# A hybrid decoder layer: four places of TensorE's planned order are made due three microseconds later

## The chip, the core and the metric

The kernel runs on one core of a Trainium2 chip. The metric is the time of one execution in microseconds of the device; lower is better. TensorE (PE in the rows) multiplies matrices, VectorE (DVE), ScalarE (ACT) and GpSimd (POOL) do the elementwise work, SyncE (SP) issues most DMAs. Weights are loaded into TensorE by a second queue, PEld.

## What is computed

One layer over 16 meta tokens and 512 tokens of 1024 channels: an RMSNorm, one projection into 11 blocks of columns, two mixers side by side, an output projection, another RMSNorm, and a mixture of 32 SwiGLU experts of which every token takes two. The first mixer is RWKV-7, a recurrence over tokens, which the kernel computes in chunks of 64 tokens:

```python
def step(S, inp):
    r_t, d_t, k_t, v_t, a_t, b_t = inp
    Sa = jnp.einsum('bhvk,bhk->bhv', S, a_t)
    S = S * d_t[:, :, None, :] + Sa[..., None] * b_t[:, :, None, :] + v_t[..., None] * k_t[:, :, None, :]
    return S, jnp.einsum('bhvk,bhk->bhv', S, r_t)
...
h = h + jnp.concatenate([y_a, y_b], axis=-1) @ w_out[l]
xn = _rmsnorm(h, norm_ffn_w[l])
h = h + _hmoe(xn, ...)     # top-1 of 4 groups, then top-2 of 8 experts, SwiGLU
```

The second mixer is an mLSTM, also in chunks. The weights of all 32 experts are read, as 16 pairs of experts with 12 tiles of 1 MB each (8 named `wgu`, 4 named `wdn`).

## The kernel before

**Stages.** (1) Projections: blocks of 128 columns, each 48 matmuls of 264 columns (three products of high and low parts, `proj_k`), in the order of `PLAN`: K, R and V blocks of the RWKV mixer (four each, numbered j = 0 to 3), then v, q, gate and o blocks of the others. (2) Between them the RWKV mixer for each j: `decays` (two groups of 6 matmuls), `norms`, `heads` (VectorE, ScalarE and GpSimd build the operands `Bbd`, `Kbd`, `MV`, one buffer of each for all four j), `products(j)` (two halves g = 0, 1 of 16 matmuls of 64x192, then two of 128x80), and `valued(j)`, which turns the values (4 matmuls of 128x128 and one of 16x128). (3) `inverse`: when the products of j = 3 are made (mark `P3`), VectorE inverts the chunks' triangles in a long row of dependent steps (`interleaved`); then TensorE does four times 32 matmuls of 32x32, two times after `need(Y2)`, two times after the copies `Zs`. (4) `chain`: nine steps over the chunks (`removals`, `solved`, `next_state`, `outputs`), with projections and the mLSTM in between. (5) The variances, the gate, the last projections (o), the output projection `w_out` (needs the token rows `x`, loaded by `residuals`), the router and the gather. (6) The experts, from L2072 on: each pair multiplies its 12 tiles as they land.

**Order.** Stages 1 to 5 are written by a planner that runs while the program is built. Each piece of work is a generator (a stream) with a rank, and `Weave.run` always resumes the stream of the lowest rank that isn't waiting. `Clock` estimates when each tensor is written; `need(...)` holds a stream back until the estimate of its operands, plus `LAG` and (for ranks above 0) `SLACK`, is reached; `bank(...)` does the same for a PSUM bank. While one stream is held back, others place their matmuls. The estimate decides only the order: on the chip each instruction waits by semaphores for what it really needs. The order of TensorE and SyncE is that in which the streams issue; the instructions of VectorE, ScalarE and GpSimd are ordered by the framework's scheduler, which sees the order of the other two. All these instructions bear line 308, that of the recording helper, so in the rows they are told apart by shape: 128x264 on arS with arR or arQ is a projection, 64x192 the products, 128x80 their last two, 128x264 on arR alone the decays, 128x128 on arF `valued` or another transposition, 32x32 the inverse.

**What hangs on the order.** The low part of each block of weights is made by VectorE until `P3` is marked and by GpSimd afterwards (`lo_by` in `prepare`). Tiles are given addresses in the arenas by the planner's clock too, and so the tiles of expert weights: `prefetch` fetches them as room appears (from the mark `var` on), `residuals` takes room for `x`, and in the experts' loop `fetch` puts each further tile into the room that has been free longest, so the tiles go round in a ring.

## Time and profile before

| | |
|---|---|
| median of 3 runs | 904.93 us (900.92 to 907.99) |
| the profiled execution | 904.07 us |
| its span, first to last instruction | 902.3 us |
| TensorE busy | 826.9 us (92%) |
| VectorE / ScalarE / GpSimd busy | 434.1 / 264.3 / 203.1 us |
| TensorE's granted clock over the span | 0.958 |
| read from HBM | 234.38 MB |

The profiled execution takes 1.8 us more than its span. A busy TensorE is one that has a matmul under way, which is not the same as one at its peak. The granted clock is a share of 2.4 GHz; the two levels are 1.0 and 0.5.

### The profile page before, as it was taken

How to read it: one execution, taken by the hardware profiler on the slowest of the kernel's cores; microseconds unless marked ns; L12 is line 12 of the kernel's file. 1: busy time of each engine (PE TensorE's matmuls, PEld its weight loads, DVE VectorE, ACT ScalarE, POOL GpSimd, SP SyncE). 2: the span in 40 equal slices, each digit the busy share in tenths (PEclk: the TensorE clock that was granted, in tenths of full speed). 3: DMA queues.
4: the chain of work that ended last, by engine and by line, in shares of the span. 5: the costliest groups of instructions: out<-in, count | busy, mean ns of one | idle time of the engine just before them, and what ended most of it. 6: DMA issues, size and time to landing. Idle time of an engine off the chain costs nothing. (4 is left out here: it accounts for less than half of the span.)

```text
span 902.3 us, 13658 instructions
## 1 busy us (share of the span) xinstructions
PE 826.9 (92%) x5487; PEld 499.0 (55%) x5488; DVE 434.1 (48%) x819; ACT 264.3 (29%) x505; POOL 203.1 (23%) x278
## 2 busy tenths in 40 slices
PE   7989697878899889999999999999999999999994
PEld 5878596777887767888343444433444423332331
DVE  7677757598746639437132333423333323331324
ACT  5755555634345584312110111001110101001102
POOL 5164625365543328220100000000000000000002
PEclk8988889988998899999999999999999999999998
DMA  6210111311300222989999999999999999999982
GB/s 238 71 42 7 47 63 55 83 34 38 102 25 2 74 84 72 386 329 348 376 406 393 419 420 420 420 420 420 420 420 420 420 421 420 420 419 422 421 349 97
DMA packets 45142, 235.60 MB, mean 261 GB/s; under 512 B 9906, under 2 KB 10290, under 8 KB 21008
## 3 DMA queue, kind: packets, MB, share of 16 engines
q1 hardware_dynamic: 42192, 228.58, 63.6%
q0 software_dynamic: 2160, 3.93, 1.1%
q10 hardware_dynamic: 720, 2.15, 0.6%
q8 instruction: 45, 0.74, 0.3%
q14 instruction: 25, 0.20, 0.1%
HBM read 234.38 MB, written 4.19 MB: 264 GB/s over the span
## 5 line engine op out<-in xcount | busy, mean ns | idle before, releaser
L308 PE MATMUL accs<-arS,arR 128*128 128x264 f32 (+2 forms) x1136 | 180.8, 311 | 8.3 <-DVE arS L308 3.5
L308 PEld LDWEIGHTS accs<-arS,arR 128*128 128x128 f32 (+1 forms) x1136 | 160.6, 199 | 22.4 <-issue 5.5
L308 PE MATMUL accs<-arF 64*64 64x192 f32 (+17 forms) x1361 | 112.6, 289 | 29.8 <-DVE arF L308 20.0
L2072 PE MATMUL accs<-arF 128*64 128x512 f32 x568 | 133.2, 599 | 6.2 <-DMA arF<-wgu 6.1
L2000 DVE TENSOR_TENSOR arF<-arF,accs 128x512 f32<-128x512 f32 x124 | 80.8, 683 | 100.4 <-PE accs L1998 98.9
L308 PEld LDWEIGHTS accs<-arF 64*64 64x64 f32 (+6 forms) x1346 | 83.1, 157 | 46.3 <-DVE arF L308 15.9
L308 POOL TENSOR_TENSOR arF<-arF 128x528 f32<-128x528 f32 (+13 forms) x97 | 89.9, 929 | 83.1 <-DVE arF L308 56.6
L1809 POOL DMA_INDIRECT arM<-hd,arF x15 | 15.1, 1008 | 372.8 <-DVE arF L1799 356.1
L308 DVE TENSOR_TENSOR arF<-arF 64x16 f32<-64x16 f32 (+31 forms) x170 | 90.2, 578 | 7.4 <-POOL arF L308 4.7
L2072 PEld LDWEIGHTS accs<-arF 128*64 128x64 f32 x568 | 37.5, 137 | 87.1 <-issue 65.3
L308 ACT ACTIVATE arF<-arF 128x528 f32<-128x528 f32 (+7 forms) x113 | 59.8, 550 | 74.7 <-DVE arF L308 51.5
L2107 ACT ACTIVATE arF<-accs,arF 128x512 f32<-128x512 f32 x16 | 11.0, 687 | 240.1 <-PE accs L2072 240.1
L308 POOL TENSOR_SCALAR arF<-arF 64x256 f32<-64x256 f32 (+9 forms) x101 | 56.9, 565 | 95.3 <-ACT arF L308 43.2
L2140 DVE SCALAR_TENSOR_TENSOR arO<-accs,arF,arO 128x1024 fp32r<-128x1024 f32 x15 | 19.3, 1284 | 103.2 <-ACT arO L2139 103.2
L2130 PE MATMUL accs<-arF 128*64 128x512 f32 x280 | 63.8, 597 | 0.2 <-DMA arF<-wdn 0.2
L1997 PE MATMUL accs<-arO,OHT 128*128 128x512 f32 x124 | 57.5, 464 | 0.0
L308 ACT COPY arF<-accs 64x256 f32<-64x256 f32 (+7 forms) x111 | 39.8, 370 | 53.8 <-PE accs L308 28.2
L308 DVE TENSOR_TENSOR arF<-accs,arF 128x128 f32<-128x128 f32 (+7 forms) x81 | 35.6, 460 | 29.0 <-PE accs L308 21.1
L1998 PE MATMUL accs<-arO,OHT 128*128 128x512 f32 x124 | 49.0, 395 | 0.0
L308 PE MATMUL accs<-arW,arS 128*128 128x512 f32 x192 | 46.7, 398 | 0.0
L1997 PEld LDWEIGHTS accs<-arO,OHT 128*128 128x128 f32 x124 | 23.3, 188 | 40.4 <-issue 38.1
L2139 ACT ACTIVATE arO<-accs,arF 128x1024 fp32r<-128x1024 f32 x15 | 16.7, 1113 | 98.7 <-PE accs L2130 98.7
(142 smaller groups left out, 930.3 us busy)
## 6 DMA issues: line engine op xcount, KB each, us to landing
arF<-wgu SPq DMA_DIRECT2D x71, 1024.0 KB, 19.8
arF<-wdn SPq DMA_DIRECT2D x35, 1024.0 KB, 19.8
arM<-wgu SPq DMA_DIRECT2D x23, 1024.0 KB, 20.0
arH<-wgu SPq DMA_DIRECT2D x17, 1024.0 KB, 19.8
arN<-wgu SPq DMA_DIRECT2D x16, 1024.0 KB, 18.6
arF<-wb SPq DMA_DIRECT2D x23, 512.0 KB, 3.6
arM<-wdn SPq DMA_DIRECT2D x10, 1024.0 KB, 20.5
arN<-wdn SPq DMA_DIRECT2D x8, 1024.0 KB, 20.4
```

The costliest lines, as they stand in the source:

```text
L308: r = f(*args, **kw)
L1809: nc.gpsimd.indirect_dma_start(out=xt[p % 2], out_offset=None, in_=hd, in_offset=bass.IndirectOffsetOnAxis(ap=idx[:, p % 2:p % 2 + 1], axi ...
L1997: P.matmul(pq, lhs, oh[:, hs], start=True, stop=False)
L1998: P.matmul(pq, lhs, ol[:, hs], start=False, stop=True)
L2000: V.tensor_tensor(hv, hv, pq, op=OP.add)
L2072: P.matmul(pgu[64 * e:64 * e + 64, h], x[:, k, 64 * e:64 * e + 64], w[:, D * e + 512 * h:D * e + 512 * h + 512], start=(k == 0), stop=(k = ...
L2107: S.activation(av, pgu[:, 0], AF.Silu, scale=r1_)
L2130: P.matmul(pdn[64 * e:64 * e + 64, h], aT[:, k, 64 * e:64 * e + 64], w[:, D * h + 512 * e:D * h + 512 * e + 512], start=(k == 0), stop=(k ...
L2139: S.activation(oh, pdf, AF.Copy, scale=g1_)
L2140: V.scalar_tensor_tensor(ol, pdf, g1_, oh.bitcast(F32), op0=OP.mult, op1=OP.subtract)
```

## The change

`need` takes an additional time, `late`, that is added to the estimate, and three callers give it `LATE = 3.0`: the values' turn in `valued`, both halves of `products`, and the first two blocks of matmuls in `inverse`. In the diff they stand in this order. `Clock` itself is not changed, so what comes behind is estimated from the later places.

```diff
+LATE = 3.0
...
-    def need(self, *aps):
+    def need(self, *aps, late=0.0):
         while True:
-            t = self.clock.wrote(*aps) + self.clock.LAG + self.slack()
+            t = self.clock.wrote(*aps) + self.clock.LAG + self.slack() + late
             if t <= self.clock.t + 0.05:
                 return
             yield t
...
-        yield from need(v)
+        yield from need(v, late=LATE)
...
-            yield from need(Bbd, Kbd, MV)
+            yield from need(Bbd, Kbd, MV, late=LATE)
...
-            yield from need(Y2)
+            yield from need(Y2, late=LATE)
```

The diff adds one line near the top, so line 308 is 309 in the changed kernel. What it does to the engines' orders is seen best at four places.

**TensorE, behind the products of j = 1.** 128x80 and 128x512 end the products and the head of j = 1; the two rows of 128x264 on arR are the decays of j = 3, 128x264 on arF is `norms`, 128x128 `valued` of j = 0, and arS with arR or arQ are projections. Before:

```order
L308 MATMUL accs<-arF 128x80 x2
L308 MATMUL accs<-arF 128x512
L308 MATMUL accs<-arR 128x264 x6
L308 MATMUL accs<-arS_68,arR 128x264 x2
L308 MATMUL accs<-arS_70,arR 128x264 x2
L308 MATMUL accs<-arS_68,arQ 128x264 x2
L308 MATMUL accs<-arR 128x264 x6
```

The changed kernel:

```order
L309 MATMUL accs<-arF 128x80 x2
L309 MATMUL accs<-arF 128x512
L309 MATMUL accs<-arR 128x264 x6
L309 MATMUL accs<-arF 128x128 x4
L309 MATMUL accs<-arF 16x128
L309 MATMUL accs<-arR 128x264 x6
```

The values' turn of j = 0 now stands between the two groups of decays; the norms of j = 3 have gone ahead of the products of j = 1.

**VectorE, at the same place.** 128x16 from accs is the last read of the bank of the 128x80 products; the 64x512 and 64x16 rows build the operands of j = 2. Before:

```order
L308 TENSOR_TENSOR arF<-accs,arF 64x16
L308 TENSOR_TENSOR arF<-arF 64x512
L308 TENSOR_TENSOR arF<-arF 64x16
L308 TENSOR_TENSOR arF<-arF 64x512
L308 TENSOR_TENSOR arF<-arF 64x16
L308 TENSOR_TENSOR arF<-accs,arF 128x16
```

The changed kernel:

```order
L309 TENSOR_TENSOR arF<-accs,arF 64x16
L309 TENSOR_TENSOR arF<-accs,arF 128x16
L309 TENSOR_TENSOR arF<-arF 64x512
L309 TENSOR_TENSOR arF<-arF 64x16
L309 TENSOR_TENSOR arF<-arF 64x512
L309 TENSOR_TENSOR arF<-arF 64x16
```

The read that frees the bank comes ahead of the four operations that build operands, no longer behind them.

**TensorE, at the inverse.** Before, 24 projections stand between its two halves:

```order
L308 MATMUL accs<-arF 32x32 x64
L308 MATMUL accs<-arS_68,arR 128x264 x2
...
L308 MATMUL accs<-arS_69,arR 128x264 x2
L308 MATMUL accs<-arF 32x32 x64
```

The changed kernel:

```order
L309 MATMUL accs<-arS_69,arR 128x264 x2
L309 MATMUL accs<-arF 32x32 x128
L309 MATMUL accs<-arS_69,arR 128x264 x2
L309 MATMUL accs<-arS_71,arR 128x264 x2
L309 MATMUL accs<-arS_69,arR 128x264 x2
L309 MATMUL accs<-arF 16x64 x8
```

The 24 projections have gone ahead of the inverse, and 6 of the 12 that stood ahead of the chain's first step (16x64) have gone behind it.

**SyncE, around the token rows.** `wgu` and `wdn` are expert weights, `wo` the output projection's, `glb` the gate's, `x` the token rows. Before:

```order
L308 DMA arF<-glb 128x512
L308 DMA arF<-glb 32x512
L308 DMA arF<-wgu 128x2048
L308 DMA arF<-wo 128x512 x10
L308 DMA arF<-x 128x1024 x4
L308 DMA arF<-wgu 128x2048 x2
```

The changed kernel:

```order
L309 DMA arF<-wgu 128x2048
L309 DMA arF<-glb 128x512
L309 DMA arF<-glb 32x512
L309 DMA arF<-wo 128x512 x10
L309 DMA arF<-wgu 128x2048 x4
L309 DMA arF<-x 128x1024 x4
```

Four tiles of expert weights go ahead of the token rows, and the first one ahead of the gate's weights. Farther down in the same queue, from the second pair of experts on, a tile's address comes back after 15 tiles in the changed kernel and after 16 before; the final norm's weights (`nlw`) and one half tile of the last pair's `wdn`, which stood at the end of the queue, stand ahead of the first pair.

Counted along TensorE's rows, from the K block of j = 2 on (behind the decays of j = 1), this many projection matmuls stand ahead of each place:

| ahead of | before | changed |
|---|---|---|
| products j = 0, first half | 48 | 54 |
| products j = 1, first half | 144 | 210 |
| products j = 2, first half | 318 | 300 |
| products j = 3, first half | 432 | 402 |
| products j = 3, last two (mark `P3`) | 474 | 432 |
| values' turn j = 3 | 564 | 576 |
| inverse, first half | 690 | 714 |
| inverse, second half | 714 | 714 |
| chain, first `removals` / first `solved` | 726 / 738 | 720 / 726 |

From the chain's second `solved` on the counts agree, and 144 projections are left when the chain is done in both.

## Rows read from the trace of the kernel before

**Rows 1.** The page's second part: TensorE's clock, the DMA engines' busy share in tenths, and what they moved, in 40 equal slices of the span (22.6 us each).

```profile
PEclk8988889988998899999999999999999999999998
DMA  6210111311300222989999999999999999999982
GB/s 238 71 42 7 47 63 55 83 34 38 102 25 2 74 84 72 386 329 348 376 406 393 419 420 420 420 420 420 420 420 420 420 421 420 420 419 422 421 349 97
```

**Rows 2.** Busy time of each engine in four stretches of the span. Columns: the stretch and its length in us; busy us (and instructions) of PE, PEld, DVE, ACT and POOL; granted clock, the DMA engines' share, GB/s.

```profile
62.00:173.00 111.00, 92.93 (x770) 80.21 (x768) 74.72 (x110) 57.81 (x114) 50.90 (x75) 0.89 0.16 54
173.00:219.00 46.00, 34.82 (x258) 32.61 (x259) 44.53 (x120) 17.93 (x45) 25.07 (x45) 0.93 0.19 51
427.00:714.00 287.00, 286.33 (x1484) 112.18 (x1482) 91.90 (x180) 31.00 (x41) 11.58 (x12) 1.00 1.01 413
714.00:870.00 156.00, 146.58 (x690) 53.34 (x688) 46.57 (x79) 14.86 (x20) 3.54 (x4) 1.00 1.01 420
```

**Rows 3.** TensorE's instructions in order of time, those that it stood idle for (and, without a wait, the norms of j = 3 at 116.46): start, duration, count, and in brackets the idle time before and the engine that ended it.

```profile
64.33 0.54 PE L308 MATMUL accs<-arF 64*64 64x192 f32 x2 [1.69 <-DVE arF L308]
66.29 3.51 PE L308 MATMUL accs<-arF 64*64 64x192 f32 x28 [1.43 <-DVE arF L308]
...
93.62 2.84 PE L308 MATMUL accs<-arF 64*64 64x192 f32 x32 [4.18 <-DVE arF L308]
108.22 0.99 PE L308 MATMUL accs<-arR 64*128 64x264 f32 x6 [1.83 <-ACT arF L308]
113.36 1.69 PE L308 MATMUL accs<-arR 64*128 64x264 f32 x6 [3.21 <-DVE arF L308]
116.46 4.05 PE L308 MATMUL accs<-arF 128*128 128x264 f32 x14
139.53 1.52 PE L308 MATMUL accs<-arF 64*64 64x192 f32 x28 [0.57 <-ACT arF L308]
144.23 1.54 PE L308 MATMUL accs<-arF 128*128 128x80 f32 x6 [1.53 <-ACT arF L308]
148.29 1.16 PE L308 MATMUL accs<-arF 128*128 128x128 f32 x8 [1.04 <-ACT arF L308]
150.87 0.57 PE L308 MATMUL accs<-arF 128*16 128x128 f32 x2 [1.42 <-DVE arF L308]
168.86 1.52 PE L308 MATMUL accs<-arF 64*64 64x192 f32 x28 [0.96 <-ACT arF L308]
175.75 1.48 PE L308 MATMUL accs<-arF 128*128 128x128 f32 x10 [2.40 <-ACT arF L308]
193.19 2.62 PE L308 MATMUL accs<-arF 128*128 128x128 f32 x10 [4.21 <-DVE arF L308]
...
218.87 3.80 PE L308 MATMUL accs<-arF 32*32 32x32 f32 x128 [3.41 <-DVE arF L308]
237.03 0.62 PE L308 MATMUL accs<-arF 64*16 64x64 f32 x16 [2.11 <-ACT arF L308]
```

**Rows 4.** The projections between 62 and 240 us, grouped: count, busy time, mean duration in ns, idle time ahead of them.

```profile
L308 PE MATMUL accs<-arS,arR 128*128 128x264 f32 x645 | 95.3, 301 | 0.7 <-POOL arR L308 0.7
L308 PE MATMUL accs<-arS,arQ 128*128 128x264 f32 x66 | 14.1, 297 | 0.0
```

**Rows 5.** VectorE in order of time behind the products of j = 1: the four 64x512 and 64x16 operations, then the read that frees the bank.

```profile
108.88 4.22 DVE L308 TENSOR_TENSOR arF<-arF 64x512 f32<-64x512 f32 x4
113.13 0.17 DVE L308 TENSOR_TENSOR arF<-accs,arF 128x16 f32<-128x16 f32 x1
```

**Rows 6.** VectorE in order of time from the end of the R block of j = 3 (its first row reads that block's sums) to the last operand of the products of j = 3.

```profile
155.19 0.71 DVE L308 TENSOR_TENSOR arF<-accs,arF 128x528 f32<-128x528 f32 x1 [1.82 <-PE accs L308]
...
157.97 0.69 DVE L308 TENSOR_TENSOR arF<-arF 128x512 f32<-128x512 f32 x1
```

**Rows 7.** ScalarE's copies `Zs` and TensorE's work between the halves of the inverse, in order of time.

```profile
224.63 1.06 ACT L308 COPY arF<-accs 32x512 f32<-32x512 f32 x2
...
222.61 4.71 PE L308 MATMUL accs<-arS,arR 128*128 128x264 f32 x24
227.25 3.80 PE L308 MATMUL accs<-arF 32*32 32x32 f32 x128
230.98 1.72 PE L308 MATMUL accs<-arS,arR 128*128 128x264 f32 x12
```

**Rows 8.** The same operation of VectorE twice, alone and beside GpSimd's copies, and one low part of a block of weights made by GpSimd within the inverse's stretch.

```profile
59.86 0.68 DVE L308 TENSOR_TENSOR arF<-arF 64x512 f32<-64x512 f32 x1 [2.84 <-POOL arF L308]
61.14 3.14 DVE L308 TENSOR_TENSOR arF<-arF 64x512 f32<-64x512 f32 x1
186.18 2.52 POOL L308 TENSOR_TENSOR arR<-arF,arR 128x1024 fp32r<-128x1024 f32 x1
```

**Rows 9.** SyncE's issues in order of time around the token rows and at the experts' start, the landing time of the token rows, and VectorE's first read of them.

```profile
359.31 1.75 SPq L308 DMA_DIRECT2D arF<-x  x4
...
469.18 0.33 SPq L1740 DMA_DIRECT2D arF<-wdn  x1
475.11 3.76 SPq L1740 DMA_DIRECT2D arF<-wgu  x3
...
DMA to landing us min/median/max: 3.5/5.5/7.4
...
379.93 0.69 DVE L308 TENSOR_TENSOR arF<-arF,accs 128x512 f32<-128x512 f32 x1 [4.95 <-PE accs L308]
```

## The prediction, made before the changed kernel ran

> **What bounds the kernel now.** I read the page's slices first [rows 1]: for the first sixteen the DMA engines are mostly idle, then they stand at 420 GB/s to the end. So the span has two parts, a front (stages 1 to 5) bound by something on the chip and the experts. The stretches tell more [rows 2]: from 427 to 714 us TensorE is busy 286.33 of 287 us, from 714 to 870 us 146.58 of 156 us with the DMA engines full. The experts are thus bound first by TensorE and later by the stream of weights. After their start each further tile is asked for when room comes free, as at 469.18 and 475.11 us [rows 9], and room comes free as pairs are multiplied; so the stream too hangs on the time at which the experts begin. I take it that a shift of the front's end passes to the end of the kernel one to one.
>
> In the front the bound is TensorE's order. From 62 to 173 us, the RWKV mixer's operands and products, TensorE is busy 92.93 of 111 us, VectorE 74.72, ScalarE 57.81 [rows 2]: no engine is full, and TensorE loses 18.1 us at waits. The order of time names them [rows 3]: products of j = 0 1.69 and 1.43, of j = 1 4.18, decays of j = 3 1.83 and 3.21, products of j = 2 0.57 and 1.53, values' turn of j = 1 1.04 and 1.42, products of j = 3 0.96, and 0.2 of small ones. From 173 us (`P3`) to the inverse at 218.87 us it is otherwise: VectorE is busy 44.53 of 46 us and TensorE 34.82 [rows 2]; the values' turns of j = 2 and 3 wait 2.40 and 4.21 us, and the inverse itself 3.41 us for VectorE [rows 3]. Behind it, `solved` waits 2.11 us at 237.03 [rows 3].
>
> **The change part by part.** No instruction is added: the same matmuls stand in another order. A projection costs (95.3 + 14.1) / (645 + 66) = 0.154 us [rows 4].
>
> *Before `P3`.* By the table of counts 432 projections stand ahead of it, 474 before: 42 fewer, -6.5 us. They go into the stretch that VectorE bounds, priced below.
>
> The waits before `P3`, one by one. Products of j = 0 have 6 more projections ahead (0.9 us): 3.1 becomes 2.1. Products of j = 1 have 66 more ahead, 10.2 us against a wait of 4.18: that wait goes. Decays of j = 3: at 113.36 us TensorE waits for the bank that VectorE reads at 113.13, behind 4.22 us of other operations [rows 5]; in the changed order that read stands ahead of the four, and the values' turn of j = 0 stands between the decays' two groups. 5.0 becomes about 1.5, the first wait, for ScalarE, less a little. Products of j = 2 and the values' turn of j = 1 get three us of the estimate more: 2.1 becomes 1.2 and 2.5 becomes 1.5, half kept, since ScalarE's and VectorE's queues aren't shorter. Products of j = 3 grow: their R block now ends only 18 projections (2.8 us) ahead of them, while its sums are read at 155.19 and the last operand is ready at 157.97 + 0.69 = 158.66 [rows 6], 3.5 us, and up to 5 us with the norms; I take 0.96 becomes 3.0. A half us for a bank and the small 0.2 stay. Together 18.1 becomes 10.0: -8.1 us. At best the waits fall to 4 (-14); at worst they all come back elsewhere (0), the first rival.
>
> *From `P3` to the inverse.* 66 projections more, 282 against 216, fill what TensorE idles there: 34.82 + 66 x 0.154 = 45.0 us of the 46 that VectorE needs. So the cover is nearly used up: whatever waits are left in the stretch beyond 1.0 us lengthen it. Of the 2.40 and 4.21 us at the values' turns I let 2 us stay, 1.0 of which shows: +1.0 us, bounds 0 and +4 (half of all waits).
>
> A price that weighs against the change: one low part of a block of weights is now made by GpSimd, for `P3` is marked earlier in the planner's order. Such a part takes 2.52 us at 186.18 us, and one operation of VectorE took 0.68 us alone and 3.14 beside GpSimd's work [rows 8]. If that befalls the inverse's steps, the stretch grows by at most 3.14 - 0.68 = 2.5 us; but GpSimd is already busy 25.07 of the 46 us there [rows 2] with VectorE's steps as long as they are, so I take 0 and keep 2.5 for the range.
>
> The Trainium skill, page *GPSIMD Engine Reference*, section "1. Specifications", says that GpSimd shares its SBUF interfaces with VectorE and that instructions of VectorE with two SBUF inputs contend with it. By it the move would cost VectorE time just where VectorE is the bound, and the sum below would end near 894 us. The two durations of rows 8 agree with the rule; that its price is paid within the inverse no row shows.
>
> *The inverse.* The 24 projections between its halves go ahead of it. That doesn't give 4.71 us [rows 7]: the second half needs ScalarE's copies, over at 224.63 + 1.06 = 225.69, and it began at 227.25. It can begin 1.6 us earlier, or 2.0 with the step of 0.4 by which the copies follow a TensorE that works on nothing else: -2.0 us, bounds 0 and -4.7.
>
> *The chain's first step.* 6 fewer projections ahead of `removals` (-0.9) and, of the 12 that stood between it and `solved`, 6 are left (12 to 6 by the table, covering a wait that is 2.11 now [rows 3]), while the 6 are done later anyway: I take +0.9 for the longer wait plus 0.8 for the rest, +1.7. Net +0.8 us. From the second `solved` on the counts agree, and so I change nothing there.
>
> *The token rows.* They are issued behind four more tiles. At 359.31 us they were issued [rows 9] and landed by 368 us, 1.75 + 7.4 later at most. Four tiles of 128 x 2048 floats (1.05 MB) take 2.5 us each at 420 GB/s [rows 1]: they land by 378 us, and VectorE first reads them at 379.93 [rows 9]. Hidden, with a margin of 2 us; without it, what is over goes to the end one to one.
>
> *The ring.* A tile's address comes back after 15 tiles, not 16, so one tile less is ahead when the experts start, and the stream is asked at 475.11 us where it was asked at 469.18 [rows 9]. The loss shows after 714 us, where the stream is the bound: one tile, +2.5 us, bounds 0 and +5.9 (the difference of the two issues).
>
> *The sum.* -6.5 - 8.1 + 1.0 - 2.0 + 0.8 + 2.5 = -12.3 us. The profiled execution took 904.07 us, 1.8 more than its span and 0.9 less than the median: 904.07 - 12.3 = 891.8, so 892 us. Bounds with the terms at their ends: 880 to 903.
>
> One gain is not in the sum. Over 62 to 173 us the granted clock is 0.89 and over 173 to 219 us 0.93 of full speed, over the experts 1.00 [rows 2]; the products before and after their waits run at such lower clock. A front with fewer gaps could get some of this back: 0.11 x 92.93 + 0.07 x 34.82 = 12.7 us is the whole of it.
>
> **The rivals.**
>
> *The waits come back.* TensorE's waits are for a chain through VectorE and ScalarE (operands of j, banks, operands of j + 1, one buffer for all four j). If this chain is what sets the time of `P3`, then taking 42 projections out just makes room for longer waits. For it: every wait in rows 3 ends on VectorE or ScalarE, and VectorE's operations stretch when GpSimd works [rows 8]. Against it: both are idle a third or half of the stretch [rows 2], and the wait at 113.36 comes from an order, not from a load [rows 5]. Then only the inverse's -2.0 and +0.8 and the ring's +2.5 are left: 904.07 + 1.3 = about 905 us.
>
> *Slower: products of j = 1 become late for all behind them.* The 66 projections more ahead of them take 10.2 us, and the norms of j = 3, also ahead now, 4.05 us at 116.46 or half of it at full clock, 2.0; against that stand 4.18 us of wait and the 1.0 saved at the products of j = 0: products of j = 1 come 7.0 us later. The operands' buffers are single, so the operands of j = 2 can be built only then; before, the products of j = 1 began at 93.62 and those of j = 2 resumed at 139.53 [rows 3], 46 us. The point from which it decides is whether this distance shrinks by those 7 us. By counts 18 projections fewer than before lie ahead of products of j = 2, so TensorE's own part of it falls by 84 x 0.154 = 12.9 us; if VectorE and ScalarE need all of the 46 us, it does not shrink, the same holds behind it, and `P3` comes 7.0 us later: 904.07 + 7.0 - 2.0 + 0.8 + 2.5 = about 912 us. Against it stands the idle third of VectorE.
>
> *More than forecast.* The sum's waits at their best (-14 for -8.1) and half of the clock's 12.7 us: 892 - 5.9 - 6.3 = about 880 us.
>
> That the change doesn't do what it says is out: the orders shown above have moved.
>
> **How the numbers follow.** Forecast near 892 us 0.50, waits back (905) 0.25, late products (912) 0.15, more gain (880) 0.10. One per cent, 9 us, is about what a measurement of this kernel can tell from no change; its bounds are 896 and 914. Faster by over 1%: four fifths of the forecast's chance and the fourth case, 0.40 + 0.10 = 0.50. Slower by over 1%: the third case where its bounds reach beyond 914 us, half of it, 0.07. The rest, 0.43, is within 1%. The range, 882 to 907 us, leaves out the third case but for its lower third (0.10), and most of the fourth (0.08): 0.18.
>
> **What would show it.** In the changed trace: products of j = 1 start with no wait; the second group of decays of j = 3 waits less than 1 us; `P3` falls near 159 us (173 less 14.6) and the inverse's first half near 205 (218.87 less 14.6, and 1.0 more); a VectorE busy nearly all of the time between; TensorE idle there under 3 us; the second half of the inverse 2 us nearer to the first; VectorE's first read of the token rows waiting for TensorE, not a DMA; the experts' start 15 us earlier, and the last pairs waiting for tiles a little more. The prediction is wrong if the distance from products of j = 1 to those of j = 2 stays 46 us, if the values' turns of j = 2 and 3 still wait for ScalarE and VectorE in a stretch that TensorE fills, or if the token rows land after 380 us less what the front gained: with the front 15 us earlier they are issued earlier too, but the four tiles ahead of them wait for room that the same front frees.

## The result, and the profile of the changed kernel

The changed kernel takes 913.58 us (median of 9 runs, 909.15 to 916.09) where the kernel before, beside it, takes 904.14: ratio 1.0112, 95% interval 1.0093 to 1.0131. It is slower by 9.4 us; faster by 12 was forecast. The profiled execution took 910.71 us, 2.9 less than the median; its span is 909.0, and so the table below accounts for 6.6 of the 9.4 us.

Where the time went is seen only when both spans are cut at the same places of the program. Each place below is the start of TensorE's first matmul there; `P3` is the end of the last products, "chain's end" that of its last matmul.

| stretch | before | changed | change | forecast |
|---|---|---|---|---|
| start to products of j = 0 | 62.10 | 60.68 | -1.4 | 0 |
| products of j = 0 to `P3` | 110.35 | 102.73 | -7.6 | -14.6 |
| `P3` to the inverse | 46.42 | 51.93 | +5.5 | +1.0 |
| first half of the inverse to the second | 8.38 | 6.33 | -2.0 | -2.0 |
| second half to the chain's first `solved` | 9.78 | 11.24 | +1.5 | +0.8 |
| chain | 72.28 | 76.48 | +4.2 | 0 |
| chain's end to the gate | 24.69 | 27.28 | +2.6 | 0 |
| gate to the output projection | 25.47 | 25.15 | -0.3 | 0 |
| output projection to the experts | 67.05 | 69.99 | +2.9 | 0 |
| experts | 475.78 | 477.19 | +1.4 | +2.5 |
| span | 902.3 | 909.0 | +6.6 | -12.3 |

At `P3` the changed kernel is 9.0 us ahead, at the chain's first step 4.1, at the chain's end level, and at the experts 5.3 behind. The stretches of the kernel before and then of the changed one (columns as in rows 2):

```profile
62.10:172.45 110.35, 92.28 (x768) 80.14 (x768) 74.44 (x109) 57.19 (x112) 50.80 (x75) 0.89 0.16 53
172.45:218.87 46.42, 35.25 (x254) 32.55 (x252) 44.58 (x121) 18.46 (x47) 25.07 (x45) 0.93 0.20 53
237.03:309.31 72.28, 66.99 (x975) 58.60 (x975) 46.99 (x94) 35.26 (x89) 30.40 (x52) 0.94 0.14 43
```

```profile
60.68:163.41 102.73, 87.59 (x720) 74.89 (x720) 73.76 (x107) 55.83 (x112) 50.75 (x75) 0.90 0.14 47
163.41:215.34 51.93, 43.12 (x321) 40.73 (x319) 46.71 (x122) 19.87 (x47) 30.23 (x47) 0.93 0.25 67
232.91:309.39 76.48, 72.25 (x1002) 63.76 (x1002) 45.88 (x96) 34.31 (x90) 29.46 (x50) 0.91 0.05 17
```

TensorE of the changed kernel in order of time, the rows that answer to [rows 3]:

```profile
101.50 1.53 PE L309 MATMUL accs<-arF 64*64 64x192 f32 x32
115.99 1.00 PE L309 MATMUL accs<-arR 64*128 64x264 f32 x6 [1.94 <-ACT arF L309]
117.31 2.61 PE L309 MATMUL accs<-arF 128*128 128x128 f32 x10 [0.32 <-DVE arF L309]
133.37 1.52 PE L309 MATMUL accs<-arF 64*64 64x192 f32 x28 [0.38 <-ACT arF L309]
151.62 2.84 PE L309 MATMUL accs<-arF 64*64 64x192 f32 x32 [3.07 <-DVE arF L309]
159.25 1.52 PE L309 MATMUL accs<-arF 64*64 64x192 f32 x28 [1.11 <-ACT arF L309]
189.85 3.87 PE L309 MATMUL accs<-arF 128*128 128x128 f32 x15 [5.20 <-DVE arF L309]
210.10 4.90 PE L309 MATMUL accs<-arS,arR 128*128 128x264 f32 x38 [2.71 <-POOL arR L309]
215.34 3.80 PE L309 MATMUL accs<-arF 32*32 32x32 f32 x128 [0.34 <-DVE arF L309]
221.67 3.83 PE L309 MATMUL accs<-arF 32*32 32x32 f32 x128 [2.53 <-ACT arF L309]
232.91 0.87 PE L309 MATMUL accs<-arF 64*16 64x64 f32 x16 [3.20 <-ACT arF L309]
336.67 0.79 PE L309 MATMUL accs<-arW 128*128 128x512 f32 x1 [6.73 <-ACT arW L309]
389.64 3.77 PE L309 MATMUL accs<-arF 128*128 128x40 f32 x32 [1.11 <-DVE arF L309]
393.23 8.08 PE L309 MATMUL accs<-arW,arS 128*128 128x512 f32 x27
```

The last three stand at the gate, at a half of the router, and at the output projection's matmuls behind it. The other engines and queues of the changed kernel at the places where it lost time:

```profile
164.85 2.39 POOL L309 TENSOR_TENSOR arR<-arF,arR 128x1024 fp32r<-128x1024 f32 x1 [9.09 <-ACT arR L309]
165.96 1.85 DVE L309 SCALAR_TENSOR_TENSOR arF<-arF 128x527 f32<-128x527 f32 x1
167.88 0.81 SPq L309 DMA_DIRECT2D arF<-eye  x2
172.69 3.68 DVE L309 TENSOR_TENSOR arF<-arF 128x31 f32<-128x31 f32 x11 [2.49 <-DMA arF<-eye]
328.83 2.96 POOL L309 TENSOR_TENSOR arW<-arF,arW 128x512 fp32r<-128x512 f32 x2
331.75 1.74 POOL L309 TENSOR_TENSOR arF<-arF 128x527 f32<-128x527 f32 x1
387.96 1.27 POOL L309 TENSOR_TENSOR arW<-arF,arW 128x512 fp32r<-128x512 f32 x1 [0.37 <-DVE arF L309]
388.42 1.16 DVE L309 TENSOR_TENSOR arF<-arF 128x320 f32<-128x320 f32 x1
```

And the kernel before at the same places:

```profile
163.43 0.75 DVE L308 SCALAR_TENSOR_TENSOR arF<-arF 128x527 f32<-128x527 f32 x1
169.89 0.82 SPq L308 DMA_DIRECT2D arF<-eye  x2
175.31 0.78 DVE L308 TENSOR_TENSOR arF<-arF 128x31 f32<-128x31 f32 x3
330.60 1.30 POOL L308 TENSOR_TENSOR arF<-arF 128x527 f32<-128x527 f32 x1 [7.73 <-DVE arF L308]
334.00 0.49 PE L308 MATMUL accs<-arW 128*128 128x512 f32 x1 [2.92 <-ACT arW L308]
385.03 0.48 DVE L308 TENSOR_TENSOR arF<-arF 128x320 f32<-128x320 f32 x1
389.16 6.50 PE L308 MATMUL accs<-arW,arS 128*128 128x512 f32 x27
```

**Three places stand out.** (1) VectorE's inverse (128x31 and its like) starts with an identity tile `XL`, which a DMA named `eye` brings. Its room was held by VectorE's mix for the V block of j = 2 (165.96), which now lies behind `P3`; the DMA was issued as that ended, and VectorE waited 2.49 us for it. The mix itself took 1.85 us beside a low part that GpSimd now makes (164.85), before 0.75 us (163.43). The inverse's steps began 9.3 us after `P3`, before 2.9 us. (2) At the gate GpSimd made two low parts of the output projection's weights (328.83) ahead of the step that the gate waits for, which began at 331.75 instead of 330.60. (3) At the router a wait of 1.11 us instead of 0.44, and then 27 matmuls in 8.08 us, before in 6.50. VectorE's step just ahead of that wait (388.42) ran beside a low part of GpSimd (387.96) and took 1.16 us, before, without one beside it, 0.48: 0.68 us, as much as the wait grew.

### The profile page after: what moved, and what is told of

The parts are those of the page before. It is cut to its first block, busy times and chain, and to the rows that moved or that the text cites. A ratio compares the mean times of both kernels' runs of the same rounds, so it can differ in the third digit from the quotient of the medians.

```text
span 909.0 us, 13652 instructions
## 1 busy us (share of the span) xinstructions
PE 829.9 (91%) x5485; PEld 499.8 (55%) x5486; DVE 435.7 (48%) x818; ACT 264.4 (29%) x505; POOL 208.0 (23%) x279
## 3 DMA queue, kind: packets, MB, share of 16 engines
q0 software_dynamic: 2160, 3.93, 1.1%
## 5 line engine op out<-in xcount | busy, mean ns | idle before, releaser
L309 PE MATMUL accs<-arF 64*64 64x192 f32 (+16 forms) x1359 | 113.0, 289 | 27.3 <-DVE arF L309 16.2
L2073 PE MATMUL accs<-arF 128*64 128x512 f32 x536 | 125.8, 600 | 5.7 <-DMA arF<-wgu 5.3
L309 POOL TENSOR_TENSOR arF<-arF 128x528 f32<-128x528 f32 (+13 forms) x97 | 95.5, 988 | 88.2 <-DVE arF L309 64.3
L1810 POOL DMA_INDIRECT arM<-hd,arF x15 | 15.1, 1007 | 374.9 <-DVE arF L1800 358.5
L2073 PEld LDWEIGHTS accs<-arF 128*64 128x64 f32 x536 | 35.0, 136 | 80.0 <-issue 58.1
L309 POOL TENSOR_SCALAR arF<-arF 64x256 f32<-64x256 f32 (+9 forms) x101 | 53.7, 534 | 88.4 <-ACT arF L309 36.3
L2131 PE MATMUL accs<-arF 128*64 128x512 f32 x272 | 61.3, 596 | 0.0
L309 PE MATMUL accs<-arW,arS 128*128 128x512 f32 x192 | 48.7, 409 | 0.6 <-ACT arF L309 0.6
L309 DVE TENSOR_TENSOR arF<-accs,arF 128x512 f32<-128x512 f32 (+7 forms) x81 | 35.5, 460 | 26.2 <-PE accs L309 15.0
L2073 PE MATMUL accs<-arM,arF 128*64 128x512 f32 x192 | 45.6, 599 | 1.7 <-DMA arM<-wgu 1.7
L309 DVE SCALAR_TENSOR_TENSOR arF<-arF 128x528 f32<-128x528 f32 (+5 forms) x50 | 35.3, 712 | 24.0 <-ACT arF L309 22.8
```

The costliest lines, as they stand in the source:

```text
L309: r = f(*args, **kw)
L1810: nc.gpsimd.indirect_dma_start(out=xt[p % 2], out_offset=None, in_=hd, in_offset=bass.IndirectOffsetOnAxis(ap=idx[:, p % 2:p % 2 + 1], axi ...
L2073: P.matmul(pgu[64 * e:64 * e + 64, h], x[:, k, 64 * e:64 * e + 64], w[:, D * e + 512 * h:D * e + 512 * h + 512], start=(k == 0), stop=(k = ...
L2131: P.matmul(pdn[64 * e:64 * e + 64, h], aT[:, k, 64 * e:64 * e + 64], w[:, D * h + 512 * e:D * h + 512 * e + 512], start=(k == 0), stop=(k ...
```

## Experiments

Most of the kernels below have **the order written down**: the turns in which the streams issued were recorded from one of the two kernels, and a fixed list replaces the planner's choice. So one thing can be changed with TensorE's and SyncE's order held. Each result gives the median, its ratio to the kernel before, run beside it, and the ratio's 95% interval; differences of a few tenths of a per cent between two such kernels are near the noise. The diffs on `TURNS` are in outline.

```diff
-class Weave:
+NAMES, TURNS = "heads chain decays ...".split(), "0 1 2 3 ...".split()
+class Weave:
```

**Which part of the order.** The cut lies in the chain, behind its sixth step: the changed order up to it and the order before behind it, and the other way round.

```diff
-TURNS = changed
+TURNS = changed[:sixth_step] + before[sixth_step:]
```

> The order of the changed kernel is kept as written down (which stream goes on at each turn) up to the chain's sixth step, the order of the kernel before stands behind it; at that point both have done the same work. In the changed kernel the chain stood 1.9 us earlier there, and the experts began 5.3 us later and took 1.4 us longer (ring of 15 tiles, which this kernel has too). Theory, the loss comes with the order behind the chain (states, outputs of the second mixer, gate): 904 - 1.9 + 1.4 = about 903.5. Rival, the loss is brought along from the front (the places in SBUF that it leaves): about 913, as the changed kernel.

Measured: 913.65 us, 1.0112 (1.0076 to 1.0147).

> The opposite cut: the order of the kernel before up to the chain's sixth step, the changed kernel's order behind it; the ring has 16 tiles. Theory, the order behind the chain loses: 904 + 7.2 = about 911. Rival, the front's places lose: about 904.

Measured: 910.84 us, 1.0071 (1.0048 to 1.0095). So the changed front loses all by itself, even with the order before behind it, and the changed rest loses too: the front's gain at `P3` was not kept by a rest that stays as it was. The two losses don't add up to that of the whole change.

**Which caller of `need`.** Each of the three with the additional time alone, then two pairs with the products. Here the planner chooses the order, as in both kernels.

```diff
-            yield from need(Bbd, Kbd, MV)
+            yield from need(Bbd, Kbd, MV, late=3.0)
```

> Only both halves of the products are due three us later, values' turns and inverse as before; the planner orders freely. Up to the last products the order on TensorE has the changed kernel's counts (432 projections ahead), the identity tile waits for the same room, the ring has 16 tiles. Theory, the products' part alone brings the gain of 8 us at the last products and the loss behind it: 908 to 913. Rival, the losses come with the later values and inverse: about 897 to 900.

Measured: 905.68 us, 1.0030 (1.0007 to 1.0054).

> Only the values' turns are due three us later; products and inverse as before, the planner orders freely. The products keep the counts of the kernel before, 6 instead of 24 projections stand between the halves of the inverse, the ring has 16 tiles. Theory, the products' part moves the front and the values alone move little: 903 to 906. Rival, the later values cost what products alone (905.7) lacks of the whole change (913.6): 908 to 912.

Measured: 904.01 us, 1.0007 (0.9987 to 1.0027).

> Only the inverse's first blocks are due three us later. Products and values keep their counts, both halves of the inverse stand behind 30 more projections (720 by the table's count), the ring has 15 tiles. Theory, TensorE works on projections while VectorE's inverse is long ready: the chain starts 30 x 0.154 less the 4.7 us between the halves, about 0 to 2 us later, and with the ring's 1.6 us: 905 to 908. Rival, the later inverse is what costs the 8 us between products alone and the whole change: 910 or more.

Measured: 905.20 us, 1.0019 (0.9997 to 1.0041).

> The whole change without its part in the inverse. By the counts 924 - 240 = 684 projections stand ahead of the inverse and 726 ahead of the chain's first next_state, as with products alone (774 in the whole change and 786 before). Theory, the inverse's late place draws 48 projections ahead of the chain's first state, which then lack as cover in the chain's waits: without it the time is that of products alone, 904 to 907. Rival, products and values together cost: 911 or more.

Measured: 906.82 us, 1.0042 (1.0020 to 1.0064).

> The whole change without its part in the values' turns: 774 projections ahead of the chain's first next_state, as in the whole change. Theory, the inverse's part turns the gain of the products into a loss: 910 to 914. Rival, it takes all three: 904 to 907.

Measured: 911.57 us, 1.0089 (1.0061 to 1.0118). By the ratios the products alone cost 2.7 us, the values 0.6, the inverse 1.7 (with the ring of 15, which costs about as much by itself, below), the last two within the noise; products and inverse together cost 8.0, and they have the ring of 15 too. The two kernels with the products late differ in the chain. Its stretch with the products alone late, and then with products and inverse late:

```profile
232.40:302.69 70.29, 66.96 (x991) 58.90 (x990) 41.44 (x87) 34.15 (x85) 31.50 (x51) 0.98 0.08 24
```

```profile
233.25:316.72 83.47, 74.81 (x1003) 65.83 (x1003) 46.09 (x97) 36.47 (x96) 30.39 (x52) 0.87 0.09 27
```

Counted along TensorE's rows, 726 projections stand ahead of the chain's first `next_state` with the products alone late, 774 with the inverse late too (and in the changed kernel), and 786 in the kernel before. The gate begins at 330.10 and at 337.45 us, 7.35 apart; 48 projections at 0.154 us [rows 4] are 7.4 us. That agreement proves little: the first of the two executions began its products of j = 0 2.3 us later (64.26 and 61.96), so from there the gates are 9.65 us apart, and the granted clock in the chain is 0.98 and 0.87. The chain's steps from the first `next_state` to the sixth `removals` behind it take about 45 us whether 126, 138 or 186 projections stand among them, so a projection inside them is hidden. That one spent before them is paid is a reading of counts and places; no run moves those 48 alone, and one run speaks against it as a rule: with the values alone late 726 stand ahead of the first `next_state` as well, the steps take 45.7 us, and yet the kernel is no faster than the one before (904.01 us), for TensorE waits 6.97 us at the gate.

**The identity tile.** The changed order written down; the two identity tiles get room by another of the planner's rules.

```diff
-        XL0 = A.get([128, 32, NM], name="XL0")
+        XL0 = A.get([128, 32, NM], name="XL0", how="group")
...
-        XL = A.get([128, 32, 32], name="XL")
+        XL = A.get([128, 32, 32], name="XL", how="group")
```

> The changed kernel with its order written down, and the two identity tiles of the inverse put into the room that is free earliest, instead of room that VectorE's mixing of V leaves at 167.80 us. Theory, the late DMA holds VectorE: its inverse starts at about 168.7 instead of 172.69, the values' turn of j = 3 waits up to 4 us less than 5.20, the inverse comes at 211.5 to 212.5 instead of 215.34, the time is 913.6 - 3 = about 910.5. Rival, TensorE and GpSimd's low parts set the inverse (TensorE waited only 0.34 us there): nothing changes, 913.6.

Measured: 907.19 us, 1.0038 (1.0011 to 1.0065): 6.4 us less than the changed kernel. In its timeline SyncE issues the tile earlier, VectorE's first step has no wait, and the matmuls at the router run as before. Between `P3` and the inverse TensorE now waits for VectorE at the values' turn (191.24) and enters the inverse, at 214.25, without a wait:

```profile
161.22 0.92 SPq L308 DMA_DIRECT2D arF<-eye  x2
166.76 1.50 DVE L308 TENSOR_TENSOR arF<-arF 128x31 f32<-128x31 f32 x1
168.18 0.75 DVE L308 SCALAR_TENSOR_TENSOR arF<-arF 128x527 f32<-128x527 f32 x1
191.24 3.88 PE L308 MATMUL accs<-arF 128*128 128x128 f32 x15 [6.10 <-DVE arF L308]
388.40 6.50 PE L308 MATMUL accs<-arW,arS 128*128 128x512 f32 x27
```

From `P3` to the inverse it takes 49.90 us instead of 51.93, the chain 75.07 instead of 76.48, and from the output projection to the experts 66.99 instead of 69.99. In the stretch where the tile is waited for, the run gains 2.0 us; the rest comes behind it, and how the tile's room brings it about isn't shown. At the router the gain isn't tied to the tile: in whole_identity_splits (below), with `XL` moved as well, the same 27 matmuls took 8.02 us.

**The gate.** Two kernels, both with the changed order written down: room for the output projection's first tiles (`wraw`) by that rule, and all first low parts by VectorE.

```diff
-            wraw.append(A.get([128, 512], name="wraw"))
+            wraw.append(A.get([128, 512], name="wraw", how="group"))
```

> The changed kernel with its order written down, and the first blocks of the output projection's weights put into the room that is free earliest. They were issued at 313.86 us (298.42 before), held by a room that the second mixer's outputs read until 313.74. Theory, the late weights push their splits on ScalarE, VectorE and GpSimd to 326 to 333 us, in front of the gate's operands: issued before 302, TensorE's wait at the gate falls from 6.73 to about 3 us, time about 910. Rival, the gate's operands are late of themselves (through GpSimd's step for block b): no change, 913.6.

Measured: 919.67 us, 1.0165 (1.0130 to 1.0200). Slower by 6 us than the changed kernel. The tiles are issued at 306.44 us, 313.86 in the changed kernel, not before 302 as the theory needed. TensorE's wait at the gate falls from 6.73 to 3.93 us, but it gets new waits ahead of it, and the gate begins at 344.34:

```profile
306.44 12.60 SPq L308 DMA_DIRECT2D arF<-wo  x4
...
318.54 0.75 PE L308 MATMUL accs<-arS,arR 128*128 128x264 f32 x4 [2.73 <-ACT arF L308]
```

Of the 7.7 us by which the gate is later, 4.0 stand ahead of the products of j = 0 already (64.67 for 60.68), and 3.2 come between the chain's end and the gate. So the run gained nothing, but whether late tiles hold the gate it neither shows nor rules out. The split:

```diff
-            split_wo(k, G if k % 2 else V)
+            split_wo(k, V)
```

> The changed kernel, its order on TensorE and SyncE written down, with the low parts of the first output weights all made by VectorE, none by GpSimd. In the changed kernel GpSimd made two of them at 328.8 to 331.8 us, ahead of its step for block b, for which the gate's last operand waits. Theory, that queue makes the gate late: GpSimd's step follows VectorE's at once, TensorE waits about 4 us at the gate instead of 6.73, time 911. Rival, ScalarE's queue (casts of the same weights, a block of o) holds the gate: no change, 913.6.

Measured: 910.91 us, 1.0073 (1.0049 to 1.0097), 2.7 less. GpSimd's step comes at once, and the wait at the gate is 3.94 us instead of 6.73:

```profile
330.15 1.31 POOL L308 TENSOR_TENSOR arF<-arF 128x527 f32<-128x527 f32 x1 [2.38 <-DVE arF L308]
334.72 0.50 PE L308 MATMUL accs<-arW 128*128 128x512 f32 x1 [3.94 <-ACT arW L308]
```

The same edit with the order before:

> The kernel before with the low parts of the first output weights on VectorE alone, its order on TensorE and SyncE written down. There GpSimd's step for block b followed VectorE's at once (330.52, 330.60), so by the theory (GpSimd's queue ahead of the gate) it gains nothing: 903 to 905. Rival, VectorE makes these parts faster whatever stands behind: 901 or less.

Measured: 901.70 us, 0.9978 (0.9958 to 0.9998): a small gain there too, of 2.0 us, though GpSimd's step followed VectorE's at once before and the wait at the gate stayed (2.96 us for 2.92). So not all of the 2.7 us need belong to GpSimd's queue.

**The ring.** The order before written down, with one tile of the gather (`xg`) at the address that the changed kernel gives it. Column 3408 of the first arena, where it lay before, is held by two tiles of the output projection at that time in the changed kernel; at 4496 it takes a slot from the ring.

```diff
-                xg.append(A.get([128, 8, 128], name="xg", how="low"))
+                xg.append(A.arenas[0].at(4496, [128, 8, 128], "xg"))
```

> The kernel before, its order written down, with one buffer (xg, the first pair's tokens) moved by 1088 columns so that it lies in the ring of the expert tiles: a tile's address comes back after 15 tiles as in the changed kernel, all else stays. Theory, a shorter ring costs time in the experts: the stretch from their start to the end grows from 475.8 by 1.4 to 3.5 us (477.2 to 479.4 in the kernels with a ring of 15 so far), so about 907. Rival, the experts were longer for other reasons: about 904.5.

Measured: 906.33 us, 1.0018 (0.9995 to 1.0040), about 1.6 us, at the edge of what can be told. The experts' stretch, which the theory put at 477.2 to 479.4 us, is 478.6.

**PSUM banks.** The changed front with the rest before, and the banks that the rest had before forced on it.

```diff
-            b = self.banks.get(n, name, among, self.clock.t - self.slack())
+            b = self.banks.get(n, name, range(same[0], same[0] + n), 1e9) if same else None
```

> As the first hybrid (the changed kernel's order up to the chain's sixth step, that of the kernel before behind it), and behind that point every stream also takes the PSUM bank that it takes in the kernel before. In the first hybrid TensorE waited 0.69 and 1.21 us there for banks that ScalarE's last gates still read, and ran slower behind it. Theory, the rotation of the banks that the changed front leaves is what loses in the chain's second half: those waits go and the gate comes about 3 us earlier, 910.5. Rival, ScalarE and VectorE are late of themselves: 913.6 as the first hybrid.

Measured: 914.67 us, 1.0123 (1.0076 to 1.0169). Then the same with the identity tile's room and the ring mended:

> The changed kernel's order up to the chain's sixth step with the identity tile put into the room that is free earliest (the ring then has 16 tiles), the order and the banks of the kernel before behind it. Theory, the front's gain was lost at the identity tile, the banks, the order behind the chain and the ring: all mended, the 4.8 to 6 us that the run with the identity tile stood ahead of the kernel before at the chain's steps reach the end: about 899. Rival, the places and queues behind the chain shift again and eat it: 904 to 907.

Measured: 909.44 us, 1.0058 (1.0037 to 1.0079). Neither theory's time came. What the banks cost by themselves the two runs don't tell, since forcing them made waits in the chain longer: in the second of these kernels 3.38 us where the kernel before has none (288.88), and 2.84 for 2.01 (306.38):

```profile
289.80 0.69 PE L308 MATMUL accs<-arF 128*128 128x128 f32 x2 [3.38 <-ACT arF L308]
310.76 1.12 PE L308 MATMUL accs<-arF 64*64 64x64 f32 x16 [2.84 <-DVE arF L308]
```

**Together.** `XL`'s room and VectorE's splits (the edits above), first in the whole changed order, with the ring of 16, and then in the order with the products alone late.

> The whole change, its order written down, with the identity tile in the room that is free earliest (the ring then has 16 tiles) and the first splits on VectorE. If the causes add: 913.6 - 6.4 (identity) - 1.6 (ring) - 2.7 (splits) = 903. If one is hidden by another: 906 to 908.

Measured: 905.27 us, 1.0013 (0.9989 to 1.0038): 8.3 of the 9.4 us are gone. The splits give the kernel before 2.0 us as well, though, so beside that kernel (901.70) some 3 us of the loss are left.

> Products alone late (its order written down), the identity tile put into the room that is free earliest, and the first splits on VectorE. Theory: 905.7 less 3 us (VectorE's inverse starts 4 us earlier, TensorE waits 5.8 us for the values' turn and 2.9 us at the inverse there) less 2 to 3 us (at the gate TensorE waited 7.4 us behind GpSimd's splits): 900. Rival, what is gained ahead of the chain's end is waited for at the gate again: 904 to 906.

Measured: 899.06 us, 0.9950 (0.9929 to 0.9971). This is faster than both kernels: 4.5 us by the ratio to the kernel before, of which the splits alone give 2.0 there. The tile's room wasn't changed in the kernel before. Its stretches from products of j = 0 to `P3`, from there to the inverse, and the chain:

```profile
61.74:163.73 101.99, 87.86 (x720) 75.22 (x720) 73.79 (x107) 55.99 (x112) 51.37 (x75) 0.90 0.16 53
163.73:213.35 49.62, 40.46 (x296) 38.01 (x294) 48.54 (x124) 18.43 (x45) 27.76 (x43) 0.90 0.23 63
229.50:301.91 72.41, 69.90 (x991) 61.34 (x990) 41.38 (x86) 34.20 (x85) 31.53 (x51) 0.93 0.08 24
```

In the profiled execution, the fastest of its eight, the gate begins at 326.49 us, 7.5 earlier than before, and the experts at 419.72, 6.8 earlier; the end is 7.5 earlier. So a shift of the experts' start does pass on to the end, as the prediction took it.

## Why the prediction was wrong

**What bounds the kernel: right.** The front's shift passes to the end. The sign was lost inside the front.

**Before `P3`: right in kind, 14.6 was 7.6.** Of the waits' 8.1 us only 2.9 came: 110.35 - 92.28 = 18.1 us became 102.73 - 87.59 = 15.1. The wait of products of j = 1 went, as said (101.50), and so did that for the bank behind the decays (115.99 and 117.31: 1.94 and 0.32 instead of 5.0). But small waits for ScalarE came in their place at the later halves of the products of j = 1, products of j = 0 kept 3.9 us where 2.1 was forecast, and products of j = 3 grew to 3.07 + 1.11 where 3.0 was forecast. The stretch holds 48 matmuls fewer, and TensorE's own work in it shrank by 92.28 - 87.59 = 4.7 us, where the prediction took 6.5 for 42 projections. Another 1.4 us came ahead of the products of j = 0; that place alone stood anywhere from 60.2 to 64.7 us in the profiled executions of these kernels, so I don't count it as a gain.

**From `P3` to the inverse: the step that failed first.** "+1.0 us, bounds 0 and +4" was +5.5. The prediction let 66 projections fill TensorE's idle time and 2 us of waits stay. TensorE's work came out near it, 43.12 us for 45.0, but the waits stayed: 51.93 - 43.12 = 8.8 us, of them 5.20 for VectorE at the values' turn (189.85) and 2.71 for a low part of GpSimd (210.10). And the prediction asked nothing of when VectorE could start. Two things moved behind `P3` with the mark: the V block's mix of 1.85 us, and with it the room of the identity tile, for which VectorE waited 2.49 us. identity_room_earlier shows what the tile's room is worth here, 2.0 us. Then TensorE reaches the inverse last, behind waits of 6.10 us for VectorE and 1.20 for GpSimd, and the stretch is still 3.5 us longer than before. The prediction went past SyncE's queue at the token rows and at the ring, and not at the inverse's own tile.

The price by which GpSimd's low part slows VectorE was put at 0, with 2.5 us kept for the range. It was paid, though not within the inverse's steps: the mix took 1.85 us beside the low part at 164.85 and 0.75 before, 1.1 us, and the identity tile's DMA came behind it. With the tile's room moved, the mix came behind the low part and took 0.75 us again (168.18), and the inverse's first step, now beside it, took 1.50 us (166.76), the like step at 168.86 0.17. The Trainium skill, page *GPSIMD Engine Reference*, section "1. Specifications", says that GpSimd shares its SBUF interfaces with VectorE and that instructions of VectorE with two SBUF inputs contend with it; these rows agree.

**The inverse's halves: right** (-2.0). **The chain's first step: small** (+1.5 for +0.8; its wait grew to 3.20 us as the cover went).

**"From the second `solved` on the counts agree, and so I change nothing there": the second step that failed**, and the dearer one: 4.2 + 2.6 - 0.3 + 2.9 = 9.4 us. Equal counts of projections don't make equal waits, for three reasons that the rows show.
- *The chain*: TensorE's work in it is 72.25 us for 66.99. It holds 27 matmuls more, 12 of them projections that stood ahead of it (1.8 us), and the granted clock is 0.91 for 0.94. The clock's part isn't settled by an experiment: no kernel holds it fixed. One row speaks for it: with the inverse alone late the chain holds 37 matmuls more than before and takes 72.50 us, at a granted clock of 1.00 (the row below this list).
- *The gate*: GpSimd's two low parts ahead of its step; first_splits_on_vector gives back 2.7 us, of which the kernel before gains 2.0 as well. Whether the late tiles themselves hold the gate stays open.
- *The router*: 0.67 us more of wait, behind a step of VectorE that GpSimd's low part lengthened by 0.68 (388.42), and 1.6 us of slower matmuls behind it (below).

```profile
237.12:309.62 72.50, 68.14 (x1012) 59.47 (x1012) 45.10 (x98) 36.90 (x104) 33.05 (x52) 1.00 0.07 24
```

A further error may lie in the sum's form; the counts suggest it, and no run isolates it. The sum took a projection away from ahead of `P3` as 0.154 us gained, wherever it went, when TensorE had room for it. The changed order puts 66 of them between `P3` and the inverse and leaves the count ahead of the chain's first `next_state` nearly as it was, 774 for 786, and at the chain the front's gain was -4.1 us. Projections that go on into the chain are hidden there. With the products alone late (726) and the two other causes mended, that became 4.5 us of gain by the ratio, 7.5 in the span of the profiled execution; with the values alone late (726 too) and nothing mended, it came to nothing.

**The sum's bounds.** With the terms at their ends the sum gives more than the 903 us named: -6.5 + 0 + 4.0 + 0 + 0.8 + 5.9 = +4.2, 908 us, and 911 with the 2.5 us kept for GpSimd. 913.58 lies beyond these as well, since all from the second `solved` to the experts was held at nothing.

**The token rows: right.** They are issued at 364.34 us, and VectorE's first read waits for TensorE:

```profile
364.34 5.42 SPq L309 DMA_DIRECT2D arF<-x  x4
383.32 1.38 DVE L309 TENSOR_TENSOR arF<-arF,accs 128x512 f32<-128x512 f32 x2 [4.95 <-PE accs L309]
```

**The ring: right.** The forecast 2.5 us were 1.4 in the stretch of the experts here, and 1.6 in the whole time and 2.8 in that stretch by before_ring_of_15. Of the eighteen kernels profiled, the nine whose tiles come back after 16 take 475.1 to 476.8 us for the experts, the nine of 15 take 477.2 to 479.3.

**The rivals.** "Late products" gave about 912 us, and 913.58 was measured, but its mechanism was not the one. It needed the distance from products of j = 1 to those of j = 2 to stay 46 us; products of j = 1 did come 7.9 us later (7.0 in the text), and the distance shrank from 45.9 to 133.37 - 101.50 = 31.9, by 14.0 us, near the 12.9 that TensorE's own part was to give. `P3` came 9.0 us earlier, not 7.0 later. A time that fits doesn't show its mechanism. "The waits come back" was right for most of the waits before `P3`; it held that nothing was lost behind. "More gain by the clock": up to `P3` the granted clock rose from 0.89 to 0.90, and in the chain it fell from 0.94 to 0.91.

**What stays open.** The three callers' single costs, 2.7, 0.6 and 1.7 us, are half of the whole's 9.4; with identity and splits mended and the ring of 16 the whole is left at a ratio of 1.0013, beside 0.9978 for the kernel before with the same splits. How the identity tile's room brings more than the 2.0 us of its own stretch isn't shown. How much of the chain's 4.2 us is the lost cover and how much the clock isn't told apart.

## What to carry to other kernels

Cut both spans at the same places of the program and carry a moved piece of work to where it ends up: it is a gain only when it leaves the critical stretches for good, not when it moves from one to the next. Where a stretch is bound by another engine, ask first when that engine can start, down to the room and the DMA of each tile that it reads. And equal counts on one engine say nothing of the waits behind them when buffers, rooms and the other engines' orders have moved.

## What the runs showed of the hardware

Operations of VectorE with two inputs took longer beside a low part that GpSimd had begun before them: 1.85 us for 0.75, 1.16 for 0.48, 1.50 for 0.17. Where VectorE began just ahead (388.26 and 388.28 us in products_and_inverse_late), its step took 0.48 us, and GpSimd's 1.61 instead of about 1.28. The 0.68 us of [rows 8] is such a case too: GpSimd began its next operation at 59.95, behind VectorE's 59.86.

Behind the wait of 1.11 us at the router the granted clock fell; the stretches of the same 27 matmuls in the changed kernel and in the one before:

```profile
393.40:401.15 7.75, 7.75 (x29) 6.09 (x28) 0.69 (x1) 0.72 (x2) 1.81 (x1) 0.78 0.93 386
```

```profile
389.40:395.50 6.10, 6.10 (x27) 4.88 (x27) 0.69 (x1) 0.72 (x2) 1.81 (x1) 1.00 1.01 422
```

In the seven kernels with a wait of over 1 us at this place the 27 matmuls took 7.86 to 9.19 us. Of the eleven with 0.44 us or none, nine took 6.49 to 6.54, but two took 8.02 and 8.07: the slower clock goes with the wait, and comes without it too, and no run changes the wait alone.

With products and inverse late the clock falls in the chain, behind waits of 3.71 and 1.21 us; three slices of 4 us, TensorE mostly idle first and then at the half level, in the last one while busy throughout.

```profile
304.00:308.00 4.00, 1.28 (x17) 1.15 (x19) 2.93 (x5) 3.89 (x17) 2.71 (x4) 0.80 0.01 2
308.00:312.00 4.00, 2.79 (x34) 2.27 (x32) 2.18 (x9) 1.51 (x8) 2.07 (x2) 0.50 0.02 4
312.00:316.00 4.00, 4.00 (x38) 3.43 (x38) 0.92 (x3) 1.09 (x6) 0.00 (x0) 0.50 0.00 0
```
